# Block two's attention with two heads at a time on the matrix engine, and the overflow path's copies on another queue

## Chip, core and metric

The kernel runs as one program on one core of a Trainium2 chip. The metric is the device time of one execution in microseconds; lower is better. Engines are named as in the profile: PE is TensorE's matmul side and PEld its weight load, DVE is VectorE, ACT is ScalarE, POOL is GpSimd, and SP is SyncE, which here only issues transfers. A "q" behind a name means the engine's sequencer.

## The reference

Two transformer blocks run one behind the other on 256 tokens of width 1024, batch 1, in float32. Block one mixes an mLSTM with a latent attention and adds a mixture of 32 experts. Block two is what the change is about. It projects the normalised tokens once, and from the pieces computes three attentions with heads of 64 columns each:

```
y_a = fox_attention(qa, ka, va, fa)                 # 4 heads, causal, logit plus sum of log f
y_b = dilated_attention(qb, kb, vb, dil_slopes)     # 6 heads in 3 groups (window, stride), joint softmax
y_c = nsa_attention(qc, kc_, vc_, ksl, vsl, kwn, vwn, gc, ...)  # 6 heads, 2 key groups: 3 parts
merged = g[0]*(y_a @ w_pa) + g[1]*(y_b @ w_pb) + g[2]*(y_c @ w_pc)
x = x + merged @ w_o
x = x + conv_ffn(rms_norm_2(x, norm2_g), w_up, conv_w, conv_b, w_down)
```

In the NSA part each head has three products of its own: selected keys, window keys, and 15 compressed keys made from blocks of 32 tokens. Each is weighted by a gate.

## The kernel before

Weights stream from HBM through rings of 1 MB tiles, all on SyncE's queue. Most products are made in three passes on rounded halves of weight and activation (lines 316, 317 and 321, or 338 to 340): ScalarE rounds a weight tile (line 300), VectorE forms the rest (line 301), TensorE multiplies. A planner puts the instructions of each engine in order by its own estimates of their times; a few orders are set by hand.

**Block one's experts** run in 8 groups of 4 (lines 1072 to 1148). Tokens above an expert's 32 places are taken by `overflow`, whose body stands under an If on the largest count (line 1247). In the measured run no expert has that many, and the body is skipped; engines pass the If all the same. Its weights come by copies that SyncE issues (line 1256), into the tiles with the tag "eo", which line 1137 also writes in the ordinary path.

**Block two's `attend`** (from line 1320) has eight PSUM banks: three with the tag "a" for projections, two "s" for scores, two "y" for outputs, one "t" for transposes and sums. `prods` loads one of 21 weight chunks and multiplies it into one "a" bank; `proj` reads the bank into queries, keys, or gates. Queries of two heads share a tile of 128 rows (64 rows each). Keys are stored twice, once for each head, with zeros in the other head's 64 rows (`kz`, `kn`; lines 1365, 1366, 1392 to 1397), so that a product over all 128 rows gives one head's scores. For each head in turn:

1. scores: a product of 128 columns and one of 256 (lines 427 and 429; for NSA's second key set lines 1596 and 1597),
2. bias or slope added by VectorE, then `softmax` (lines 438 to 446) on VectorE and ScalarE,
3. `turn`: three transposes (line 454) into the "t" bank and one copy by ScalarE (line 455),
4. `pv`: the values' products (lines 459 and 460) into 64 of the 128 rows of a "y" bank.

There are 4 such heads for FoX, 6 for dilated (all scores of three groups for one half first, then one softmax over them) and 6 for NSA, which pass steps 1 to 4 for two key sets each: 22 passes of steps 3 and 4. Chunks 11 to 20 of the projection don't depend on the attention and are placed by the planner between its steps; the last two (`LATE`) stand by hand behind the last NSA score product (`tc.issue_after`, line 1643). The merged projections (`wp`) and the output projection (`wo2`) follow, then `ffn`.

Of the kernel before, what the change touches and what calls it, by code (L numbers as in the profile page):

```python
# [222 lines left out]
class Prog:  # L223
# [1016 lines left out]
    def overflow(self, tm, pm, psum, hn, W, pos, thr, most):  # L1240
# [6 lines left out]
        with tc.If(most > CAP, preferred_fallthrough_block=False):  # L1247
# [72 lines left out]
    def attend(self, ei):  # L1320
# [12 lines left out]
        def mps(tag, bufs):  # L1333
            return psum("a", 3)
# [11 lines left out]
        parts = [psum("s", 2) for _ in range(2)]  # L1346
# [4 lines left out]
        pt = psum("t", 1)  # L1351
# [9 lines left out]
        kz = pa.tile([P, 5, 2, T], F32, name="kz")  # L1361
        kn = pa.tile([P, 2, 527], F32, name="kn")
        for p in range(2):
            o = slice(64 * (1 - p), 64 * (1 - p) + 64)
            g.memset(kz[o, :, p], 0.0)
            g.memset(kn[o, p], 0.0)

        def prods(ch, h):
            w = self.load(I["w2a"][ch] if ch < 20 else I["w2a1"][0])
            if ch == CAT:  # L1370
                self.const(self.pc, "tab2", ["pos0", "dil00", "cmp0", "cmp1", "cval0", "hsel", "wfg", "ck2", "cv2"] +
                           [f"dil{i}0" for i in range(3)], nc.sync)
                self.rows(self.pc, "row2", ["bv", "bfg"], nc.sync)
                self.const(self.pc, "tri", ["negu", "cmask"], nc.sync)
            pp = psum("a", 3)
            for j in range(w.shape[-1] // D):
                self.tile_a(w[:, j * 1024:(j + 1) * 1024], h, [(pp[:, j * T:(j + 1) * T], 0, KD)])
            return pp

        def place(n, o):  # L1380
            b = self.co("b2", n, 1)
            lo, up = slice(0, 64), slice(64, 128)
            if n < 2:
                for gi, r in enumerate((lo, up)):
                    a.activation(zt[lo, 2 * n + gi], o[r], AF.Identity, bias=b[r])
                    a.activation(zt[up, 2 * n + gi, 0:T - 1], o[r, 1:T], AF.Identity, bias=b[r])
            elif n in (2, 3, 6, 7, 8, 12, 13, 14):
                i = {2: 0, 3: 1, 6: 2, 7: 3, 8: 4, 12: 5, 13: 6, 14: 7}[n]
                a.activation(q_[:, i], o, AF.Identity, bias=bs[:, n:n + 1], scale=0.125)
            elif n in (4, 5, 9, 10, 11):  # L1390
                i = {4: 0, 5: 1, 9: 2, 10: 3, 11: 4}[n]
                v.tensor_scalar(out=kz[lo, i, 0], in0=o[lo], scalar1=b[lo], scalar2=None, op0=OP.add)
                v.tensor_scalar(out=kz[up, i, 1], in0=o[up], scalar1=b[up], scalar2=None, op0=OP.add)
            elif n in (15, 16):
                s = slice(0, 256) if n == 15 else slice(271, 527)
                v.tensor_scalar(out=kn[lo, 0, s], in0=o[lo], scalar1=b[lo], scalar2=None, op0=OP.add)
                v.tensor_scalar(out=kn[up, 1, s], in0=o[up], scalar1=b[up], scalar2=None, op0=OP.add)
            else:
                a.activation(gates[:, n - 17], o, AF.Tanh, bias=bh[:, n - 17:n - 16], scale=0.5)
# [76 lines left out]
        for kv in range(2):  # L1476
# [7 lines left out]
            part = psum("a", 3)  # L1484
# [9 lines left out]
            hp = psum("a", 3)  # L1494
# [10 lines left out]
            if kv == 0:  # L1505
                v.scalar_tensor_tensor(out=hu, in0=hu, scalar=1.0, in1=hx, op0=OP.add, op1=OP.mult)
                kp = psum("a", 3)
# [3 lines left out]
                for gi in range(2):  # L1511
                    r = slice(64 * gi, 64 * gi + 64)
                    v.tensor_scalar(out=kn[r, gi, 256:271], in0=kp[r, 0:NCMP], scalar1=0.5, scalar2=None, op0=OP.mult)
            else:
# [4 lines left out]
                vp = psum("a", 3)  # L1519
# [7 lines left out]
        gb = [psum("s", 2) for _ in range(2)]  # L1527
# [13 lines left out]
        def finish(Pn, yo, vs):  # L1541
            PT = tm.tile([P, 384], F32, name="PT", tag="PT")
            self.turn(Pn, psum("t", 1), PT)
            self.pv(yo, V[:, 0, vs], V[:, 1, vs], PT)

        for i in range(2):
            yp = psum("y", 2)
            for p in range(2):
                hd = 2 * i + p
                S = psum("s", 2)  # L1550
                self.scores(S, [(q_[:, i], kz[:, i, p])])
                Pn = tm.tile([P, 384], F32, name="Pn", tag="Pn")
                v.tensor_tensor(out=Pn, in0=S[:, 0:384], in1=mc[:, hd], op=OP.add)
                self.softmax(Pn, Pn, sm)
                finish(Pn, yp[64 * p:64 * p + 64], slice(hd * 64, hd * 64 + 64))
            self.hilo(yp[:, :T], y[0][:, i], y[1][:, i])
# [3 lines left out]
        halves = (slice(0, 128), slice(128, 384))  # L1560
        for p in range(2):
            Pd = tm.tile([P, 3, 384], F32, name="Pd", tag="big6", bufs=1)
            for gi in range(3):
                S = psum("s", 2)
                self.scores(S, [(q_[:, 2 + gi], kz[:, 2 + gi, p])])
                at = COLS[f"dil{gi}0"][0]
                v.scalar_tensor_tensor(out=Pd[:, gi], in0=self.where["dil00"][:, at:at + 384], scalar=DIL_SLOPES[gi * 2 + p],
                                       in1=S[:, 0:384], op0=OP.mult, op1=OP.add)
            cc = sm.tile([P, 6], F32, name="smc", tag="smc")
            for q, s in enumerate(halves):  # L1570
                v.tensor_reduce(out=cc[:, q:q + 1], in_=Pd[:, :, s], axis=AX.XY, op=OP.max, negate=True)
            for q, s in enumerate(halves):
                a.activation(Pd[:, :, s], Pd[:, :, s], AF.Exp, bias=cc[:, q:q + 1], accum_out=cc[:, 2 + q:3 + q])
            v.tensor_scalar(out=cc[:, 2:4], in0=cc[:, 2:4], scalar1=TINY, scalar2=None, op0=OP.max)
            v.reciprocal(out=cc[:, 4:6], in_=cc[:, 2:4])
            for q, s in enumerate(halves):
                v.tensor_scalar(out=Pd[:, :, s], in0=Pd[:, :, s], scalar1=cc[:, 4 + q:5 + q], scalar2=None, op0=OP.mult)
            for gi in range(3):
                hd = 2 * gi + p
                finish(Pd[:, gi], yp[gi // 2][64 * p:64 * p + 64, (gi % 2) * T:(gi % 2 + 1) * T], slice(512 + hd * 64, 576 + hd * 64))  # L1580
# [8 lines left out]
        for i in range(3):  # L1589
            yp = psum("y", 2)  # L1590
            for gi in range(2):
                hd = i + 3 * gi
                q = q_[:, 5 + i]
                S1, S2 = psum("s", 2), psum("s", 2)
                self.scores(S1, [(q, kn[:, gi, 0:256])])
                mm(S2[:, 0:143], q[:, 0:128], kn[:, gi, 256:399], start=True, stop=True)
                late = mm(S2[:, 143:414], q[:, 128:256], kn[:, gi, 256:527], start=True, stop=True)
                sl = NSA_SLOPES[hd]
                Pn = [tm.tile([P, 384], F32, name="Pn", tag="Pn") for _ in range(2)]
                v.scalar_tensor_tensor(out=Pn[0], in0=pos, scalar=sl, in1=S1[:, 0:384], op0=OP.mult, op1=OP.add)  # L1600
                v.scalar_tensor_tensor(out=Pn[1][:, 0:128], in0=pos[:, 0:128], scalar=sl, in1=S2[:, 15:143], op0=OP.mult, op1=OP.add)
                v.scalar_tensor_tensor(out=Pn[1][:, 128:384], in0=pos[:, 128:384], scalar=sl, in1=S2[:, 158:414], op0=OP.mult, op1=OP.add)
                for qq in range(2):
                    v.scalar_tensor_tensor(out=Pc[:, qq, hd * 15:hd * 15 + 15], in0=self.co(f"cmp{qq}"), scalar=sl,
                                           in1=S2[:, 143 * qq:143 * qq + 15], op0=OP.mult, op1=OP.add)
                yo = yp[64 * gi:64 * gi + 64, :T]
                for b in range(2):
                    self.softmax(Pn[b], Pn[b], sm, gc[:, :, hd * 3 + 1 + b])
                    PT = tm.tile([P, 384], F32, name="PT", tag="PT")
                    self.turn(Pn[b], psum("t", 1), PT)  # L1610
                    vs = 256 + 128 * b + 64 * gi
                    self.pv(yo, V[:, 0, vs:vs + 64], V[:, 1, vs:vs + 64], PT, first=b == 0, last=b == 1)
# [14 lines left out]
        tp = psum("t", 1)  # L1627
# [37 lines left out]
        part = psum("s", 2)  # L1665
        for ch in range(4):
            w = self.load(I["wo2"][ch])
            pp = psum("a", 3)
# [7 lines left out]
        self.sumcol(psum("t", 1), [(part, 4, D)], cols[:, 56:58], tm)  # L1676
# [137 lines left out]
```

## Time and profile before

| | |
|---|---|
| median of 3 runs | 1019.4 us (1016.81 to 1020.24) |
| profiled execution | 1018.99 us |
| its span | 1017.1 us |
| mean granted TensorE clock | 0.970 |
| PE busy | 946.8 us, 93% of the span |
| DVE busy | 611.6 us, 60% |
| ACT busy | 475.4 us, 47% |

The profiled execution is one of its own and not one of the three runs. Busy times of engines overlap, and their shares are means over stages with different limits. In block two the attention lies from about 644 to 760 us of the span, between the first projections (from 556) and the merged ones.

### The profile page before, as it was taken

The page shows a single profiled execution, that of the slowest core. Times are in us where ns is not written, and L with a number is a line of the kernel's source. Part 1 is how long each engine was busy: PE and PEld are TensorE (multiplying, and loading weights), DVE is VectorE, ACT ScalarE, POOL GpSimd, SP SyncE. Part 2 cuts the span into 40 slices and gives each one's busy share as a digit, 9 for nine tenths or more (in the row PEclk, how much of TensorE's full clock was granted, in tenths as well). Part 3 has the DMA queues.
Part 4 walks back from the last instruction along what each step waited for, and adds up shares of the span by engine and source line. Part 5 has one row for each costly group of instructions (what it writes and reads, how often), then busy time and mean ns, then how long its engine had stood idle before and what let it go on. Part 6 is the DMA issues. An engine that isn't in the chain of part 4 may idle for free.

```text
span 1017.1 us, 17796 instructions
## 1 busy us (share of the span) xinstructions
PE 946.8 (93%) x6870; PEld 774.7 (76%) x6870; DVE 611.6 (60%) x1471; ACT 475.4 (47%) x1017; POOL 16.7 (2%) x32
## 2 busy tenths in 40 slices
PE   5899899999999899997598999999999999999995
PEld 2678888999998554443243998789879799999994
DVE  3468699654763423242134884756779688676764
ACT  3446766455542222120114754656654565555553
POOL 0000000000000000000010000000002000000001
PEclk9899899999999799998799999999999999999998
DMA  8967367669568599999899555723324444554501
GB/s 359 399 277 275 119 248 267 231 266 421 183 239 354 201 423 411 419 422 419 351 380 420 224 187 186 271 103 123 127 83 165 148 166 166 172 201 167 200 8 43
DMA packets 37388, 249.77 MB, mean 246 GB/s; under 512 B 4272, under 2 KB 5040, under 8 KB 8368
## 3 DMA queue, kind: packets, MB, share of 16 engines
q1 hardware_dynamic: 37008, 248.01, 63.2%
q8 instruction: 56, 0.92, 0.4%
q10 hardware_dynamic: 288, 0.55, 0.2%
q14 instruction: 36, 0.29, 0.1%
HBM read 247.49 MB, written 1.05 MB: 244 GB/s over the span
## 4 chain that ended last, share of the span: by engine, by line
PE 45%; ACT 2%; DVE 2%; issue 1%; ACTq 0%; DVEq 0%
PE ps_a L316 9%; PE ps_a L317 9%; PE ps_a L321 9%; PE ps_acc L1772 6%; PE ps_gu L1089 1%; PE ps_y L459 1%; PE ps_c L1131 1%; PE ps_dn L1148 1%; PE ps_t L454 1%; PE ps_a L339 1%; PE ps_a L338 1%; PE ps_a L340 1%; PE ps_s L429 1%; PE ps_y L460 0%; PE ps_a L1489 0%
## 5 line engine op out<-in xcount | busy, mean ns | idle before, releaser
L301 DVE TENSOR_TENSOR wlo<-w,whi 128x512 fp32r<-128x512 f32 (+2 forms) x426 | 288.7, 685 | 151.5 <-ACT whi L300 134.9
L300 ACT CAST whi<-w 128x512 fp32r<-128x512 f32 (+2 forms) x426 | 258.1, 611 | 249.8 <-PE ps_a L317 189.4
L316 PE MATMUL ps_a<-hh,whi 128*128 128x256 f32 x304 | 79.9, 294 | 4.9 <-ACT hh L612 3.1
L317 PE MATMUL ps_a<-hl,whi 128*128 128x256 f32 x304 | 79.4, 291 | 0.0
L1132 DVE SCALAR_TENSOR_TENSOR xT<-ps_c,modc,xT 128x256 f32<-128x256 f32 x72 | 33.1, 483 | 72.5 <-PE ps_c L1131 72.3
L316 PE MATMUL ps_a<-h4h,whi 128*128 128x256 f32 x304 | 76.1, 283 | 0.2 <-ACT h4h L343 0.2
L317 PE MATMUL ps_a<-h4l,whi 128*128 128x256 f32 x304 | 76.1, 283 | 0.0
L1089 PE MATMUL ps_gu<-w,xg 128*32 128x512 f32 x512 | 68.8, 618 | 6.5 <-issue 6.5
L316 PEld LDWEIGHTS ps_a<-hh,whi 128*128 128x128 f32 x304 | 60.0, 198 | 9.1 <-ACT hh L612 3.3
L316 PE MATMUL ps_a<-h2h,whi 128*128 128x256 f32 x248 | 63.9, 288 | 0.0
L317 PE MATMUL ps_a<-h2l,whi 128*128 128x256 f32 x248 | 63.6, 287 | 0.0
L317 PEld LDWEIGHTS ps_a<-hl,whi 128*128 128x128 f32 x304 | 60.2, 198 | 2.0 <-issue 1.2
L316 PEld LDWEIGHTS ps_a<-h4h,whi 128*128 128x128 f32 x304 | 58.1, 192 | 1.2 <-ACT h4h L343 0.6
L317 PEld LDWEIGHTS ps_a<-h4l,whi 128*128 128x128 f32 x304 | 58.1, 192 | 0.3
L1131 PE MATMUL ps_c<-PT,eo 128*128 128x256 f32 (+1 forms) x144 | 41.9, 410 | 12.9 <-ACT eo L1137 11.8
L1131 PEld LDWEIGHTS ps_c<-PT,eo 128*128 128x128 f32 (+1 forms) x144 | 24.3, 192 | 37.1 <-ACT eo L1137 16.1
L1072 PEld LDWEIGHTS ps_x<-Ph,hn 128*128 128x128 f32 x256 | 34.1, 199 | 22.4 <-issue 17.6
L321 PE MATMUL ps_a<-hh,wlo 128*128 128x256 f32 x304 | 49.3, 285 | 0.0
L321 PE MATMUL ps_a<-h4h,wlo 128*128 128x256 f32 x304 | 48.7, 283 | 0.0
L316 PEld LDWEIGHTS ps_a<-h2h,whi 128*128 128x128 f32 x248 | 47.4, 191 | 0.7 <-issue 0.4
L1077 ACT ACTIVATE xg<-ps_x,modc,cols 128x128 f32<-128x128 f32 x32 | 14.6, 457 | 70.6 <-PE ps_x L1072 61.1
L317 PEld LDWEIGHTS ps_a<-h2l,whi 128*128 128x128 f32 x248 | 47.4, 191 | 0.2
(521 smaller groups left out, 2049.1 us busy)
## 6 DMA issues: line engine op xcount, KB each, us to landing
w<-in_egu_dram SPq DMA_DIRECT2D x66, 1024.0 KB, 18.4
w<-in_edn_dram SPq DMA_DIRECT2D x33, 1024.0 KB, 19.8
w<-in_up_dram SPq DMA_DIRECT2D x22, 1024.0 KB, 4.7
w<-in_w2a_dram SPq DMA_DIRECT2D x20, 1024.0 KB, 7.0
w<-in_mod_dram SPq DMA_DIRECT2D x19, 1024.0 KB, 7.5
w<-in_win_og_dram SPq DMA_DIRECT2D x12, 1024.0 KB, 6.5
w<-in_dn_dram SPq DMA_DIRECT2D x11, 1024.0 KB, 4.8
w<-in_br_dram SPq DMA_DIRECT2D x8, 1024.0 KB, 12.6
```

The costliest lines, as they stand in the source:

```text
L300: nc.scalar.copy(hi, src)
L301: nc.vector.tensor_tensor(out=lo, in0=src, in1=hi.bitcast(F32), op=OP.subtract)
L316: mm(out, hi[:, s], ah[:, k], start=first, stop=False)
L317: mm(out, hi[:, s], al[:, k], start=False, stop=False)
L321: mm(out, lo[:, s], ah[:, k], start=False, stop=last)
L338: mm(out, ah[:, k, ts], hi[:, s], start=a, stop=False)
L1072: mm(o[:, i * P:(i + 1) * P], hn[:, q, d * P:(d + 1) * P], Phs[b][q], start=q == 0, stop=q == 1)
L1077: a.activation(xgs[0][:, i], o[:, i * P:(i + 1) * P], AF.Identity, scale=ac[:, d:d + 1], bias=modc[:, 24 + d:25 + d])
L1089: mm(gu[32 * j:32 * j + 32], xgs[d // 4][:, d % 4, j * CAP:(j + 1) * CAP], w[:, j * 512:(j + 1) * 512], start=d == 0, stop=d == KD - 1)
L1131: mm(o[:, i * T:(i + 1) * T], eo_[:, (d0 + i) * P:(d0 + i + 1) * P], PT, start=True, stop=True)
L1132: v.scalar_tensor_tensor(out=xT[:, d], in0=o[:, i * T:(i + 1) * T], scalar=g2[:, d:d + 1], in1=xT[:, d], op0=OP.mult, op1=OP.add)
L1772: mm(acc[q][nh], x[:, q * P:(q + 1) * P], y, start=k == 0 and x is ah and y is hi, stop=k == KF - 1 and y is lo)
```

## The change

Heads are handled two at a time. Keys are stored once, without zeros. `scores2` takes two heads' products from the two halves of rows into two banks of one tile. `finish2` transposes both heads into a tile of two banks, copies both with one ScalarE instruction of 768 columns, and issues the values' products of both heads next to each other, each to its half of the output's rows. NSA computes the scores of both heads for the first key set, then of both for the second, then the four softmaxes; `late` is now the last product of the second set. The dilated scores of all groups and both halves go to one tile before the softmaxes.

The tags of banks change: "a" has two banks (each `psum("a", 3)` in `attend` becomes `psum("a", 2)`), "s" and "t" are one tile of two banks each, "y" still has two. Small users move: sums of squares, `gb` and the merged projection's third bank to "s", the last sums to "t" and "y". In `overflow` the weight copies are issued by ScalarE (`a`) instead of SyncE.

```diff
@@ overflow @@
                     def part(name, i):
                         w = tm.tile([P, 512], F32, name="wp", tag="eo")
-                        nc.sync.dma_start(w, self.I[name].rearrange("b i p (j f) -> b j i p f", j=4)[bass.ds(b, 1), j, i]
-                                          .rearrange("o p f -> (o p) f"))
+                        a.dma_start(w, self.I[name].rearrange("b i p (j f) -> b j i p f", j=4)[bass.ds(b, 1), j, i]
+                                    .rearrange("o p f -> (o p) f"))
                         return w
@@ attend @@
+        def psum2(tag):
+            return ps.tile([P, 2, 512], F32, name="ps_" + tag, tag=tag, bufs=1)
...
-        kz = pa.tile([P, 5, 2, T], F32, name="kz")
-        kn = pa.tile([P, 2, 527], F32, name="kn")
-        for p in range(2):
-            o = slice(64 * (1 - p), 64 * (1 - p) + 64)
-            g.memset(kz[o, :, p], 0.0)
-            g.memset(kn[o, p], 0.0)
+        k_ = pa.tile([P, 5, T], F32, name="k_")
+        kn = pa.tile([P, 527], F32, name="kn")
...
-                v.tensor_scalar(out=kz[lo, i, 0], in0=o[lo], scalar1=b[lo], scalar2=None, op0=OP.add)
-                v.tensor_scalar(out=kz[up, i, 1], in0=o[up], scalar1=b[up], scalar2=None, op0=OP.add)
+                v.tensor_scalar(out=k_[:, i], in0=o, scalar1=b, scalar2=None, op0=OP.add)
...
-            outs = [psum("a", 3)[:, :n1 - n0] for _ in range(2)]
+            outs = [psum("a", 2)[:, :n1 - n0] for _ in range(2)]
...
-        def finish(Pn, yo, vs):
-            PT = tm.tile([P, 384], F32, name="PT", tag="PT")
-            self.turn(Pn, psum("t", 1), PT)
-            self.pv(yo, V[:, 0, vs], V[:, 1, vs], PT)
+        rows = (slice(0, 64), slice(64, 128))
+
+        def scores2(q, k, w0=128, w1=256):
+
+            S = psum2("s")
+            for p, r in enumerate(rows):
+                mm(S[:, p, 0:w0], q[r, 0:128], k[r, 0:w0], start=True, stop=True)
+            for p, r in enumerate(rows):
+                x = mm(S[:, p, w0:w0 + w1], q[r, 128:256], k[r, 0:w1], start=True, stop=True)
+            return S, x
+
+        def finish2(Ps, yo, vs, first=True, last=True):
+            tp = psum2("t")
+            for p in range(2):
+                for j in range(3):
+                    te.transpose(tp[:, p, j * P:(j + 1) * P], Ps[p][:, j * P:(j + 1) * P], self.co("ident"))
+            PT = tm.tile([P, 2, 384], F32, name="PT", tag="PT")
+            a.copy(PT, tp[:, :, 0:384])
+            for p, r in enumerate(rows):
+                mm(yo[r, 0:256], V[:, 0, vs + 64 * p:vs + 64 * p + 64], PT[:, p, 0:256], start=first, stop=False)
+            for p, r in enumerate(rows):
+                mm(yo[r, 128:256], V[:, 1, vs + 64 * p:vs + 64 * p + 64], PT[:, p, 256:384], start=False, stop=last)
...
+            q = q_[:, 5 + i]
+            S, _ = scores2(q, kn)
+            Ps = [[tm.tile([P, 384], F32, name="Pn", tag="Pn", bufs=4) for _ in range(2)] for _ in range(2)]
+            for gi in range(2):
+                v.scalar_tensor_tensor(out=Ps[0][gi], in0=pos, scalar=NSA_SLOPES[i + 3 * gi], in1=S[:, gi, 0:384], op0=OP.mult, op1=OP.add)
+            S, late = scores2(q, kn[:, 256:527], 143, 271)
...
+            for b in range(2):
+                for gi in range(2):
+                    hd = i + 3 * gi
+                    self.softmax(Ps[b][gi], Ps[b][gi], sm, gc[:, :, hd * 3 + 1 + b])
+                finish2(Ps[b], yp, 256 + 128 * b, first=b == 0, last=b == 1)
...
-            pp = [psum("a", 3) for _ in range(3)]
+            pp = [psum("a", 2) for _ in range(2)] + [psum2("s")[:, 0]]
```

## Rows read from the trace of the kernel before

**Rows 1.** The page: busy time of each engine, and the chain by engine
```profile
PE 946.8 (93%) x6870; PEld 774.7 (76%) x6870; DVE 611.6 (60%) x1471; ACT 475.4 (47%) x1017; POOL 16.7 (2%) x32
...
PE 45%; ACT 2%; DVE 2%; issue 1%; ACTq 0%; DVEq 0%
```

**Rows 2.** Table by stage: length, busy us of PE, PEld, DVE, ACT, POOL, clock, DMA share
```profile
572.00:600.00 28.00, 28.00 (x236) 28.00 (x236) 27.70 (x71) 19.95 (x42) 0.00 (x0) 1.00 0.40 140
...
664.00:690.00 26.00, 26.00 (x195) 23.57 (x194) 14.99 (x32) 13.84 (x28) 0.00 (x0) 1.00 0.29 101
...
712.00:760.00 48.00, 46.56 (x328) 38.97 (x328) 34.94 (x122) 29.16 (x83) 0.00 (x0) 1.00 0.32 112
```

**Rows 3.** TensorE's instructions by line, 644 to 760 us: count, busy us, mean ns
```profile
L459 PE MATMUL ps_y<-PT,V 128*64 128x256 f32 x44 | 14.2, 405 | 1.0 <-ACT PT L455 0.9
...
L429 PE MATMUL ps_s<-kz,q__5882 128*128 128x256 f32 x20 | 6.0, 380 | 0.0
```

**Rows 4.** TensorE's timeline at one head of NSA: start, duration, line, count
```profile
717.85 0.28 PE L316 MATMUL ps_a<-h2h,whi 128*128 128x256 f32 x1
717.97 0.28 PE L317 MATMUL ps_a<-h2l,whi 128*128 128x256 f32 x1
718.18 0.65 PE L459 MATMUL ps_y<-PT,V 128*64 128x256 f32 x2
...
718.98 0.51 PE L1596 MATMUL ps_s<-kn,q__5882 128*128 128x143 f32 x2
```

**Rows 5.** Chain of work from 757 to 761 us: start, duration, line, count
```profile
758.60 0.68 PE ps_y L1635 x4
```

**Rows 6.** TensorE's timeline at two score products, 662 and 728 us
```profile
662.57 0.39 PE L427 MATMUL ps_s<-kz,q__5882 128*128 128x128 f32 x2
...
663.22 0.33 PE L1521 MATMUL ps_a<-tab,hv 128*128 128x64 f32 x2
...
728.55 0.40 PE L1596 MATMUL ps_s<-kn,q__5882 128*128 128x143 f32 x2
...
729.37 0.27 PE L317 MATMUL ps_a<-h2l,whi 128*128 128x256 f32 x1
```

**Rows 7.** Timeline at 570 us; TensorE at 624 us; line 1467 (ns min/median/max, starts)
```profile
569.95 0.28 PE L316 MATMUL ps_a<-h0h,whi 128*128 128x256 f32 x1
...
570.90 0.60 PE L407 MATMUL ps_t<-tab,nc 128*128 128x128 f32 x4
...
572.84 1.41 DVE L1431 TENSOR_TENSOR os<-ps_a,rr 128x256 f32<-128x256 f32 x4
...
624.25 0.33 PE L338 MATMUL ps_a<-whi,h2h 128*128 128x384 f32 x1
...
L1467 DVE TENSOR_TENSOR V<-ps_a,row x4: 548/620/692, 624.2 to 635.5; 128x512 f32<-128x512 f32 x2, 128x384 f32<-128x384 f32 x2
```

**Rows 8.** VectorE's and ScalarE's instructions by line, 644 to 760 us
```profile
L438 DVE TENSOR_REDUCE smc<-Pn 128x1 f32<-128x128 f32 (+1 forms) x32 | 9.9, 344 | 0.1
L446 DVE TENSOR_SCALAR Pn<-Pn,smc 128x128 f32<-128x128 f32 (+1 forms) x32 | 8.7, 315 | 0.2
...
L455 ACT COPY PT<-ps_t 128x384 f32<-128x384 f32 x22 | 10.5, 478 | 17.1 <-PE ps_t L454 17.1
```

**Rows 9.** VectorE's instructions by line, 556 to 640 us
```profile
L1393 DVE TENSOR_SCALAR kz<-os,small 64x256 f32<-64x256 f32 x3 | 1.1, 354 | 0.0
```

**Rows 10.** What the If's line 1247 issues: ns min/median/max, first to last start
```profile
L1247 SPq EVENT_SEMAPHORE  x8: 17/17/17, 488.4 to 507.0; - x8
...
L1247 ACTq EVENT_SEMAPHORE  x1: 17/17/17, 463.9 to 463.9; - x1
```

**Rows 11.** ScalarE's timeline behind the If; in brackets the idle time before
```profile
480.82 0.46 ACT L1077 ACTIVATE xg<-ps_x,modc,cols 128x128 f32<-128x128 f32 x1 [17.02 <-PE ps_x L1072]
...
504.66 0.58 ACT L1137 COPY eo<-ps_dn 128x512 f32<-128x512 f32 x1 [13.04 <-SPq L1247]
```

**Rows 12.** Engines and DMA from 504 to 512 us
```profile
504.00:512.00 8.00, 6.71 (x29) 3.19 (x30) 2.22 (x5) 1.63 (x3) 0.00 (x0) 0.72 0.25 70
```

More of the change, by code (lines that the diff above doesn't have):

```diff
@@ L1345, in attend @@
         h0 = act("h0")
-        parts = [psum("s", 2) for _ in range(2)]
+        parts = psum2("s")
+        parts = [parts[:, i] for i in range(2)]
         sq8 = pa.tile([P, 24, T], F32, name="sq8", tag="gt")
@@ L1391, in place @@
                 i = {4: 0, 5: 1, 9: 2, 10: 3, 11: 4}[n]
-                v.tensor_scalar(out=kz[lo, i, 0], in0=o[lo], scalar1=b[lo], scalar2=None, op0=OP.add)
-                v.tensor_scalar(out=kz[up, i, 1], in0=o[up], scalar1=b[up], scalar2=None, op0=OP.add)
+                v.tensor_scalar(out=k_[:, i], in0=o, scalar1=b, scalar2=None, op0=OP.add)
             elif n in (15, 16):
                 s = slice(0, 256) if n == 15 else slice(271, 527)
-                v.tensor_scalar(out=kn[lo, 0, s], in0=o[lo], scalar1=b[lo], scalar2=None, op0=OP.add)
-                v.tensor_scalar(out=kn[up, 1, s], in0=o[up], scalar1=b[up], scalar2=None, op0=OP.add)
+                v.tensor_scalar(out=kn[:, s], in0=o, scalar1=b, scalar2=None, op0=OP.add)
             else:
@@ L1483, in attend @@
                         in1=self.co("pe", 8 * hf2, 8).unsqueeze(2).to_broadcast([P, 8, NCMP]), op=OP.add)
-            part = psum("a", 3)
+            part = psum("a", 2)
             for hf2 in range(2):
@@ L1493, in attend @@
             proj(9 + kv, h)
-            hp = psum("a", 3)
+            hp = psum("a", 2)
             for hh in range(2):
@@ L1510, in attend @@
                         mm(kp[64 * gi:64 * gi + 64, 0:NCMP], self.co("ck2", hh * 64, 64), hu[:, hh, gi], start=hh == 0, stop=hh == 1)
-                for gi in range(2):
-                    r = slice(64 * gi, 64 * gi + 64)
-                    v.tensor_scalar(out=kn[r, gi, 256:271], in0=kp[r, 0:NCMP], scalar1=0.5, scalar2=None, op0=OP.mult)
+                v.tensor_scalar(out=kn[:, 256:271], in0=kp[:, 0:NCMP], scalar1=0.5, scalar2=None, op0=OP.mult)
             else:
@@ L1525, in attend @@
         y = act("y2")
-        gb = [psum("s", 2) for _ in range(2)]
+        gb = psum2("s")
+        gb = [gb[:, i] for i in range(2)]
         mc = pa.tile([P, 4, 384], F32, name="mc", tag="zm")
@@ L1539, in attend @@
             a.copy(es2[:, :, 128:256], gs[:, :, 0:128])
-        def finish(Pn, yo, vs):
-            PT = tm.tile([P, 384], F32, name="PT", tag="PT")
-            self.turn(Pn, psum("t", 1), PT)
-            self.pv(yo, V[:, 0, vs], V[:, 1, vs], PT)
+        rows = (slice(0, 64), slice(64, 128))
[17 more added lines that the diff above has]
+                mm(yo[r, 128:256], V[:, 1, vs + 64 * p:vs + 64 * p + 64], PT[:, p, 256:384], start=False, stop=last)
         for i in range(2):
             yp = psum("y", 2)
+            S, _ = scores2(q_[:, i], k_[:, i])
+            Ps = [tm.tile([P, 384], F32, name="Pn", tag="Pn", bufs=4) for _ in range(2)]
             for p in range(2):
[L1549 to L1555, printed above, removed]
+                v.tensor_tensor(out=Ps[p], in0=S[:, p, 0:384], in1=mc[:, 2 * i + p], op=OP.add)
+                self.softmax(Ps[p], Ps[p], sm)
+            finish2(Ps, yp, 128 * i)
             self.hilo(yp[:, :T], y[0][:, i], y[1][:, i])
@@ L1560, in attend @@
         halves = (slice(0, 128), slice(128, 384))
-        for p in range(2):
[L1562 to L1568, printed above, removed]
+        Pd = tm.tile([P, 2, 3, 384], F32, name="Pd", tag="big6", bufs=1)
+        for gi in range(3):
+            S, _ = scores2(q_[:, 2 + gi], k_[:, 2 + gi])
+            at = COLS[f"dil{gi}0"][0]
+            for p in range(2):
+                v.scalar_tensor_tensor(out=Pd[:, p, gi], in0=self.where["dil00"][:, at:at + 384], scalar=DIL_SLOPES[gi * 2 + p],
+                                       in1=S[:, p, 0:384], op0=OP.mult, op1=OP.add)
+        for p in range(2):
             cc = sm.tile([P, 6], F32, name="smc", tag="smc")
             for q, s in enumerate(halves):
-                v.tensor_reduce(out=cc[:, q:q + 1], in_=Pd[:, :, s], axis=AX.XY, op=OP.max, negate=True)
+                v.tensor_reduce(out=cc[:, q:q + 1], in_=Pd[:, p, :, s], axis=AX.XY, op=OP.max, negate=True)
             for q, s in enumerate(halves):
-                a.activation(Pd[:, :, s], Pd[:, :, s], AF.Exp, bias=cc[:, q:q + 1], accum_out=cc[:, 2 + q:3 + q])
+                a.activation(Pd[:, p, :, s], Pd[:, p, :, s], AF.Exp, bias=cc[:, q:q + 1], accum_out=cc[:, 2 + q:3 + q])
             v.tensor_scalar(out=cc[:, 2:4], in0=cc[:, 2:4], scalar1=TINY, scalar2=None, op0=OP.max)
@@ L1576, in attend @@
             for q, s in enumerate(halves):
[L1577 to L1580, printed above, removed]
+                v.tensor_scalar(out=Pd[:, p, :, s], in0=Pd[:, p, :, s], scalar1=cc[:, 4 + q:5 + q], scalar2=None, op0=OP.mult)
+        for gi in range(3):
+            finish2([Pd[:, p, gi] for p in range(2)], yp[gi // 2][:, (gi % 2) * T:(gi % 2 + 1) * T], 512 + 128 * gi)
         self.hilo(yp[0].rearrange("p (j t) -> p j t", j=2), y[0][:, 2:4], y[1][:, 2:4])
@@ L1594, in attend @@
[L1594 to L1597, printed above, removed]
                 sl = NSA_SLOPES[hd]
-                Pn = [tm.tile([P, 384], F32, name="Pn", tag="Pn") for _ in range(2)]
-                v.scalar_tensor_tensor(out=Pn[0], in0=pos, scalar=sl, in1=S1[:, 0:384], op0=OP.mult, op1=OP.add)
@@ L1601, in attend @@
-                v.scalar_tensor_tensor(out=Pn[1][:, 0:128], in0=pos[:, 0:128], scalar=sl, in1=S2[:, 15:143], op0=OP.mult, op1=OP.add)
-                v.scalar_tensor_tensor(out=Pn[1][:, 128:384], in0=pos[:, 128:384], scalar=sl, in1=S2[:, 158:414], op0=OP.mult, op1=OP.add)
+                Pw, Sw = Ps[1][gi], S[:, gi]
+                v.scalar_tensor_tensor(out=Pw[:, 0:128], in0=pos[:, 0:128], scalar=sl, in1=Sw[:, 15:143], op0=OP.mult, op1=OP.add)
+                v.scalar_tensor_tensor(out=Pw[:, 128:384], in0=pos[:, 128:384], scalar=sl, in1=Sw[:, 158:414], op0=OP.mult, op1=OP.add)
@@ L1603, in attend @@
                 for qq in range(2):
                     v.scalar_tensor_tensor(out=Pc[:, qq, hd * 15:hd * 15 + 15], in0=self.co(f"cmp{qq}"), scalar=sl,
[L1605 to L1612, printed above, removed]
+                                           in1=Sw[:, 143 * qq:143 * qq + 15], op0=OP.mult, op1=OP.add)
@@ L1664, in attend @@
         self.h0 = act("h3")
-        part = psum("s", 2)
+        part = psum2("t")[:, 0]
         for ch in range(4):
             w = self.load(I["wo2"][ch])
-            pp = psum("a", 3)
+            pp = psum("a", 2)
             for j in range(2):
@@ L1675, in attend @@
                 self.scaled(self.h0, xT, n, hc)
-        self.sumcol(psum("t", 1), [(part, 4, D)], cols[:, 56:58], tm)
+        self.sumcol(psum("y", 2), [(part, 4, D)], cols[:, 56:58], tm)
     def ffn(self, eo):
```

13 lines of the change are left out of this document (6 added, 7 removed).

## The prediction

> **What bounds the kernel now.** I began with the page's busy times and chain: TensorE is busy 946.8 of 1017.1 us, and the chain that ended last is nearly all TensorE [rows 1]. So an edit pays if it takes time off TensorE where TensorE sets the pace, and costs if it makes TensorE wait. The table by stage then says where that is. In block two's attention (644 to 760 us) TensorE is at 26.00 of 26 us and 46.56 of 48, VectorE and ScalarE far below it [rows 2]. In the projections ahead of it (572 to 600) TensorE has 28.00 of 28, with VectorE at 27.70 close behind. Third, TensorE's lines and its own timeline gave counts and prices of the small products [rows 3 to 6]. Last I looked at the two places where the change moves something else: the turn of the projection's banks near 570 us [rows 7], and the If of the overflow path near 490 us [rows 10 to 12]. All prices are from the one profiled execution, 1018.99 us, which is 0.4 us below the median of 1019.4; the sum is taken from the execution and the forecast put on the median.
>
> **Values' products.** Before, each of 22 heads (NSA's six count twice, once for each key set) issues two matmuls of line 459 and two records of line 460 (x44 is 22 times two [rows 3]). In the timeline the last projection matmul starts at 717.97; such matmuls follow one another at 0.12 us, so the next would start at 718.09, but line 459 starts at 718.18, and the next full-width matmul at 718.98 [rows 4]. One head thus takes 0.89 us of TensorE, 0.09 of it on entering the narrow form. The change issues both heads of a pair next to each other, one on each half of the columns. The trace has that form already: line 1635, two heads on two column halves, four records in 0.68 us [rows 5], where two records of one head last 0.65 [rows 4]. So the second head is nearly free. I take 11 pairs at 0.89 in place of 22 heads: 19.6 to 9.8, **-9.8 us**. If the halves ran one after the other the second head would save only its change of form, 11 times 0.09 or -1; line 1635 speaks against that.
>
> The Trainium skill, "TensorEngine Tiling (Array Packing)", section "Key Properties", says that a change of tiling mode drains TensorE. It speaks against many short stretches of narrow matmuls, and the trace agrees: the 0.09 us on the way in [rows 4].
>
> **Scores.** Sixteen heads (4 FoX, 6 dilated, 6 NSA) take 662.57 to 663.22, 0.65 us each. The second NSA product starts at 728.55; the second projection matmul behind it starts at 729.37, which without the break would be 0.12 after the first, so the pair of products took 729.25 - 728.55 = 0.70 us [rows 6], six times. Together 14.6 us. Before, half of each contraction was zeros; after, two heads stand on two halves of rows, into two banks. No row of this trace has two row halves side by side. Two bounds: side by side, a pair costs one head plus a change of form in and out, about 0.2 (twice the 0.09 of rows 4): 8 x 0.85 + 3 x 0.90 = 9.5, **-5.1 us**; one after the other, 14.6 + 11 x 0.2 = 16.8, +2.2 us. The nearest row is line 1635, the same array cut the other way, which does overlap; I take -5.1.
>
> The Trainium skill, "TensorE: Matmul & The Clock Gate", section "Part 3: Packing small matmuls", says that matmuls on different row groups run concurrently, 3.07 times as fast for four of them. No run here shows it yet; by it the scores would save the -5.1, without it they lose the 2.2.
>
> **One copy for two heads.** The transposes stay (66 of them). ScalarE's 22 copies of line 455, 478 ns each, become 11 of twice the width [rows 8]. ScalarE has 29.16 of 48 us there [rows 2], so this lies beside TensorE: 0.
>
> **What the pair gives back.** Both heads' softmaxes must now be done before a pair's transposes, the scores have one pair of banks instead of two single ones, and the last two projection chunks, held behind the last NSA score, must cover four softmaxes where they covered two. A softmax costs VectorE two reductions of 344 ns and two scalings of 315, 1.3 us [rows 8]. Two more behind the last score are 2.6 us; the wider copy adds up to 0.5 and the second head's reads of the scores about 0.4 by the nearest of these rows. The cover is two chunks; in the stage before, TensorE idles only 1.4 us of 48. I take **+3.5**. Nothing if the chunks still cover it all; at most 9, if all three NSA pairs pay about 3.
>
> **Banks: three to two.** The projections now turn over two banks. At the start, the third chunk's first matmul runs at 569.95, into the third bank; chunk zero's bank is read by line 1431 only from 572.84, two of its four instructions of 0.35 us, so it is free at 573.5 [rows 7]. With two banks TensorE would stand 3.6 us; line 407 and its row of sums can move up into the gap, since TensorE's queue would no longer hold matmuls ahead of it (at most some 1.3 us). I take +2.6. In V, the second pair of groups starts at 624.25, while line 1467 only begins to read the first pair at 624.2, 620 ns each [rows 7]: +0.8 for what it would wait. Elsewhere (compression, merged projections) one short read each: +0.6. Together **+4.0**, bounds 2 to 7.
>
> **Keys without padding.** Each key tile loses one of two writes of 64 partitions (354 ns [rows 9]) and GpSimd its memsets. TensorE is full in that stretch, so 0; at best 1 us, as VectorE is at 27.70 of 28 [rows 2].
>
> **The overflow path's queue.** The body isn't run, but its If is passed. At its line SyncE's queue carries eight semaphore events from 488.4 to 507.0, every other engine that works in the body one, at once [rows 10]. ScalarE's copy of line 1137 waits 13.04 us for them, to 504.66 [rows 11], and TensorE behind it. From 504 to 512 DMA is busy for a quarter of the time, so some 6 us of its 8 are lost [rows 12]. In my forecast the eight stay where they are, or wait just as long elsewhere with nobody behind them that is later than today: 0.
>
> **Sum.** -9.8 - 5.1 + 3.5 + 4.0 = -7.4 us: 1018.99 to 1011.6, on the median **1012.0 us**. With the bounds of the give-backs this case has its own range, 1007 to 1017.
>
> **Rivals.**
> *ScalarE waits at the If (slower).* The eight events stood on the queue that issues the body's copies; that queue is now ScalarE's. ScalarE reached the If near 463.9 [rows 10] and would stand there to 507.0. Its work that began at 480.82 then begins 26 us later; the copy at 504.66 came 23.8 us behind that work's start, 13.04 of it waiting, so it would come at 507.0 + 10.8 + up to 1.5 = 519.3, some 14.6 late. Less up to 3 where TensorE waits anyhow behind it, about +12 (between +5, if weights that land meanwhile let TensorE catch up, and +15). With -7.4: 1024 us. For it: the events sit on the issuing queue today. Against: they may be placed by something else than the queue. It decides the sign from 7.4 us of lateness on.
> *SyncE is freed and nobody waits.* The weights keep flowing across the If, and the lost 6 us [rows 12] come off the block: 1006. Against it: TensorE, not DMA, may set the pace behind the If.
> *Row halves run one after the other.* Scores +2.2 instead of -5.1: 1019, no change.
> *The attention's chain takes it back.* VectorE's part of both heads and the single pair of banks cost the upper 9, banks 5: 1019 - 14.9 + 14 = about 1018.
>
> **Chances.** Forecast 0.40; ScalarE waits 0.30; SyncE freed 0.10; row halves 0.09; chain 0.11. Below 0.3%, 3 us, a measurement of this kernel can't tell a change from none. Faster: 0.37 of the forecast, all 0.10 of SyncE freed, 0.05 of the last two: 0.52. Same: 0.03, 0.04 of the slower rival's low end, 0.11 of the last two: 0.18. Slower: 0.26 and 0.04: 0.30. The range runs from 1006 (SyncE freed) to 1026 (the upper part of the slower rival).
>
> **What would show it.** In the new trace, TensorE's two heads of line 459's successor should span about what one spanned, 0.89 us a pair; the score pair about 0.85; a TensorE wait of 2 to 3 us near 570; a few us of wait at the end of attention; and at the If either eight events on SyncE as today, or on ScalarE with a wait to 507. Score pairs of 1.5 us, or ScalarE idle from 464 to 507, would make the prediction wrong.

## The result and the profile after

The changed kernel takes 1007.0 us (median of 4 runs, 1003.45 to 1009.55) against 1018.11 before on the same chip: ratio 0.9889, 95% interval 0.9871 to 0.9907. Run again later beside the experiments it gave 1008.54 us and 0.9907 (0.9890 to 0.9923). I take the mean of the two ratios, 0.9898, as the measure for the experiments: 10.4 us of 1018. Its profiled execution took 1006.2 us with a span of 1004.4, where that of the kernel before had 1017.1.

The page's busy times, which answer to [rows 1]:

```profile
PE 928.5 (92%) x6870; PEld 761.9 (76%) x6870; DVE 604.9 (60%) x1463; ACT 473.3 (47%) x1006; POOL 13.0 (1%) x28
```

TensorE has as many instructions as before and is busy 18.3 us less. Where, by line, in the attention (count, busy us, mean ns; [rows 3] before):

```profile
L1559 PE MATMUL ps_y<-PT,V 128*64 128x256 f32 x44 | 7.2, 405 | 0.3 <-ACT PT L1557 0.3
L1548 PE MATMUL ps_s<-kn,q__5881 64*128 64x256 f32 (+1 forms) x24 | 4.4, 387 | 0.0
...
L1548 PE MATMUL ps_s<-k__5882,q__5881 64*128 64x256 f32 x20 | 3.0, 377 | 0.0
```

The mean of one of the 44 products of line 1559 is the same 405 ns as before, but together they fill 7.2 us where they filled 14.2: they run side by side. The same holds for the row halves of the scores, which the trace of before couldn't show (20 records of 377 ns in 3.0 us, where [rows 3] has 20 of 380 in 6.0). TensorE's timeline gives the price of a pair:

```profile
659.82 0.65 PE L1559 MATMUL ps_y<-PT,V 128*64 128x256 f32 x4 [0.26 <-ACT PT L1557]
660.31 0.39 PE L1561 MATMUL ps_y<-PT,V 128*64 128x128 f32 x4
660.63 0.87 PE L1555 MATMUL ps_t<-tab,Pn 128*128 128x128 f32 x6
661.43 0.49 PE L1546 MATMUL ps_s<-k__5882,q__5881 64*128 64x128 f32 x4
661.75 0.60 PE L1548 MATMUL ps_s<-k__5882,q__5881 64*128 64x256 f32 x4
662.29 0.43 PE L1517 MATMUL ps_a<-tab,hv 128*128 128x64 f32 x2
```

Two heads' values take 659.82 to 660.63, 0.81 us, and one head took 718.18 to 718.98, 0.80 [rows 4]. Two heads' scores take 661.43 to 662.29, 0.86 us, and one took 0.65 [rows 6], so two took 1.30.

The attention also ends earlier within its stage. Before, the last addition of NSA's parts (line 1636) stood behind the last projection, and the last score product (line 1597) 11 us ahead of that projection's end:

```profile
739.98 0.62 PE L1597 MATMUL ps_s<-kn,q__5882 128*128 128x271 f32 x2
...
751.43 0.64 PE L321 MATMUL ps_a<-h2h,wlo 128*128 128x256 f32 x4
```
```profile
L1636 DVE TENSOR_TENSOR yc<-yc,ps_y x3: 415/420/421, 759.3 to 760.5; 128x256 f32<-128x256 f32 x3
```

Now the last addition (line 1648, 737.4) stands ahead of the last projection (742.73), and the last score product 30 us ahead of it:

```profile
712.54 0.72 PE L1548 MATMUL ps_s<-kn,q__5881 64*128 64x271 f32 x2
```
```profile
L1648 DVE TENSOR_TENSOR yc<-yc,ps_y x3: 420/420/422, 733.6 to 737.4; 128x256 f32<-128x256 f32 x3
```
```profile
742.73 0.64 PE L321 MATMUL ps_a<-h2h,wlo 128*128 128x256 f32 x4
743.21 0.28 PE L316 MATMUL ps_s<-y2h,whi 128*128 128x256 f32 x1
```

The wait that two banks cost at the first turn (the third chunk's first matmul, [rows 7]) with the read that it waits for, and the If ([rows 10]):

```profile
571.52 0.36 PE L316 MATMUL ps_a<-h0h,whi 128*128 128x256 f32 x1 [1.34 <-DVE os L1429]
```
```profile
570.63 1.41 DVE L1429 TENSOR_TENSOR os<-ps_a,rr 128x256 f32<-128x256 f32 x4
```
```profile
L1247 SPq EVENT_SEMAPHORE  x8: 17/17/17, 487.8 to 506.0; - x8
...
L1247 ACTq EVENT_SEMAPHORE  x1: 17/17/17, 463.0 to 463.0; - x1
```

The eight events are on SyncE still, though the body's copies are now issued by ScalarE, which passes the If at 463.0 (463.9 before).

How much TensorE works and how much it waits, in three stretches of both kernels: from 556 us to the first score product of the attention, on to the end of the attention (behind its last addition before, behind the last projection now), and on to the sums of the norm ahead of `ffn`. First before, then now (columns as in [rows 2]):

```profile
556.00:645.00 89.00, 88.51 (x679) 82.11 (x677) 66.80 (x158) 53.13 (x107) 0.00 (x0) 1.00 0.60 221
645.00:762.00 117.00, 114.42 (x846) 98.25 (x844) 79.57 (x246) 68.81 (x179) 0.00 (x0) 1.00 0.35 127
762.00:812.60 50.60, 48.35 (x365) 43.42 (x365) 41.37 (x67) 27.15 (x51) 6.06 (x7) 1.00 0.45 157
```
```profile
556.00:645.10 89.10, 86.97 (x676) 81.85 (x676) 62.65 (x150) 52.27 (x106) 0.00 (x0) 1.00 0.54 202
645.10:743.20 98.10, 95.53 (x809) 82.77 (x809) 74.79 (x239) 64.87 (x166) 0.00 (x0) 1.00 0.40 142
743.20:799.90 56.70, 52.08 (x402) 47.50 (x400) 43.35 (x70) 28.97 (x55) 5.60 (x7) 1.00 0.48 165
```

The whole way is 256.6 us before and 243.9 now: all of the 12.7 us between the two executions lie here. TensorE's busy time fell by 16.7 us (251.3 to 234.6). Its waits, the rest of each stretch, grew by 4.0: from 0.5 to 2.1 in the projections, from 2.2 to 4.6 behind the attention, and not at all in the attention (2.6 in both).

### The profile page after: what moved, and what is told of

Read it like the earlier page. It is cut to its first block, busy times and chain, and to the rows that moved or that the text cites. A ratio compares the mean times of both kernels' runs of the same rounds, so it can differ in the third digit from the quotient of the medians.

```text
span 1004.4 us, 17784 instructions
## 1 busy us (share of the span) xinstructions
PE 928.5 (92%) x6870; PEld 761.9 (76%) x6870; DVE 604.9 (60%) x1463; ACT 473.3 (47%) x1006; POOL 13.0 (1%) x28
```

## The experiments

Ratios are to the kernel before, with 95% intervals; the changed kernel's is 0.9898.

**Scores of both heads on one row half.**

```diff
-                mm(S[:, p, 0:w0], q[r, 0:128], k[r, 0:w0], start=True, stop=True)
+                mm(S[:, p, 0:w0], q[rows[0], 0:128], k[rows[0], 0:w0], start=True, stop=True)
...
-                x = mm(S[:, p, w0:w0 + w1], q[r, 128:256], k[r, 0:w1], start=True, stop=True)
+                x = mm(S[:, p, w0:w0 + w1], q[rows[0], 128:256], k[rows[0], 0:w1], start=True, stop=True)
```

> The changed kernel, but both heads of a score pair read the same half of rows (0 to 64) of queries and keys, so head 1 gets head 0's scores: as many matmuls of the same shapes, only not on two halves. If the gain is TensorE's own time, the pairs no longer run side by side and the scores cost what the other bound of the prediction said, 16.8 us in place of 9.5: 7 us slower than the changed kernel, about 4 below the kernel before. If the gain came from the chain of softmaxes and copies, TensorE's extra time hides and it stays 11 below.

Ratio 0.9946 (0.9931 to 0.9961), 4.9 us slower than the changed kernel. TensorE's timeline in this run:

```profile
662.31 0.71 PE L1546 MATMUL ps_s<-k__5882,q__5881 64*128 64x128 f32 x4
662.86 1.03 PE L1548 MATMUL ps_s<-k__5882,q__5881 64*128 64x256 f32 x4
663.82 0.43 PE L1517 MATMUL ps_a<-tab,hv 128*128 128x64 f32 x2
```

A pair now takes 1.51 us instead of 0.86. Eleven pairs are 7.2 us of TensorE's time, most of which is in the end time. The array's time decides, not the chain. This run is not the kernel before at that place: two heads took 1.30 us there, not 1.51, so its 4.9 us can't be read as the pairing's gain.

**Values' products head by head.**

```diff
-            for p in range(2):
+            PT = tm.tile([P, 2, 384], F32, name="PT", tag="PT")
+            for p, r in enumerate(rows):
                 for j in range(3):
                     te.transpose(tp[:, p, j * P:(j + 1) * P], Ps[p][:, j * P:(j + 1) * P], self.co("ident"))
-            PT = tm.tile([P, 2, 384], F32, name="PT", tag="PT")
-            a.copy(PT, tp[:, :, 0:384])
-            for p, r in enumerate(rows):
+                a.copy(PT[:, p], tp[:, p, 0:384])
                 mm(yo[r, 0:256], V[:, 0, vs + 64 * p:vs + 64 * p + 64], PT[:, p, 0:256], start=first, stop=False)
-            for p, r in enumerate(rows):
                 mm(yo[r, 128:256], V[:, 1, vs + 64 * p:vs + 64 * p + 64], PT[:, p, 256:384], start=False, stop=last)
```

> The changed kernel with the values' products head by head: transposes, a copy of 384 columns and both products of head 0, then the same for head 1; score pairs and banks as changed. If the gain is TensorE's time, 22 times 0.89 us return in place of 11: 9.8 us slower than the changed kernel, about 1 below the kernel before. If what counts is that both heads' softmaxes and copies overlap, which stays, it is within 3 us of the changed kernel.

Ratio 0.9988 (0.9975 to 1.0000), 9.2 us slower than the changed kernel. The products fill 14.2 us again:

```profile
L1558 PE MATMUL ps_y<-PT,V 128*64 128x256 f32 x44 | 14.2, 405 | 1.0 <-ACT PT L1557 1.0
```

**One copy per head, and two copies cut by columns.** The run above also splits ScalarE's copy, so two controls split it alone.

```diff
-            a.copy(PT, tp[:, :, 0:384])
+            for p in range(2):
+                a.copy(PT[:, p], tp[:, p, 0:384])
```

> The changed kernel with two ScalarE copies of 384 columns per pair in place of one of 768; products still paired. The control for the run with the products head by head: if that run lost TensorE's time, this one stays within 2 us of the changed kernel. If it lost by the chain through ScalarE's copies, this one loses several us too.

Ratio 0.9962 (0.9947 to 0.9976): 6.5 us slower. By its time alone that is the second case, the chain through ScalarE. But the trace shows that most of the products weren't paired any more; in seven of the eleven pairs a projection matmul stands between the two heads, as here:

```profile
L1560 PE MATMUL ps_y<-PT,V 128*64 128x256 f32 x44 | 12.0, 405 | 0.0
```
```profile
696.84 0.65 PE L1560 MATMUL ps_y<-PT,V 128*64 128x256 f32 x2
697.41 0.38 PE L317 MATMUL ps_a<-h2l,whi 128*128 128x256 f32 x1
697.73 0.43 PE L1560 MATMUL ps_y<-PT,V 128*64 128x256 f32 x1
```

The likely reason is that with a copy per head the first head is ready first by the planner's times, so that the planner fills the time between. So a second control:

```diff
-            a.copy(PT, tp[:, :, 0:384])
+            a.copy(PT[:, :, 0:256], tp[:, :, 0:256])
+            a.copy(PT[:, :, 256:384], tp[:, :, 256:384])
```

> The changed kernel with two copies per pair again, but cut by columns: the first brings 256 columns of both heads, the second 128, so both heads' products become ready together and stand next to each other on TensorE in the planned order. If the run with one copy per head lost 6 us because the planner set the products of a pair apart, this one stays within 2 us of the changed kernel. If a second copy's time on ScalarE costs it, this one is some 6 us slower too.

Ratio 0.9891 (0.9876 to 0.9906), that of the changed kernel, with the products at 7.2 us again. The number of copies costs nothing that can be seen; what cost the 6.5 us is that the two heads no longer stood next to each other on TensorE.

**Two projection banks in the kernel before.**

```diff
-            pp = psum("a", 3)
+            pp = psum("a", 2)
...
-            pp = [psum("a", 3) for _ in range(3)]
+            pp = [psum("a", 2) for _ in range(2)] + [psum("s", 2)]
```

> The kernel before with two projection banks in place of three (the merged projection's third bank from the scores' tag) and nothing else. By the prediction's term 4.0 us slower than before (2.6 at the first turn, 0.8 in V, 0.6 elsewhere). By what the changed kernel's trace shows (a wait of 1.34 us at the first turn, V some 1 us late) about 2. A rival: the planner fills the gap with other work and it costs nothing that can be measured.

Ratio 1.0033 (1.0021 to 1.0045): 3.4 us slower, 2.1 to 4.6 by the interval. The third case is out; 4.0 fits, and 2 isn't far outside. TensorE's waits in this run:

```profile
570.29 0.35 PE L316 MATMUL ps_a<-h0h,whi 128*128 128x256 f32 x1 [1.34 <-DVE os L1431]
...
783.32 0.55 PE L316 MATMUL ps_a<-mg2h,whi 128*128 128x256 f32 x1 [3.37 <-DVE mm L1657]
```

1.34 us at the first turn, and 3.37 behind the merged projection, a place to which the prediction had given a part of 0.6. The kernel before waited 0.69 us in that stage:

```profile
775.91 0.36 PE L316 MATMUL ps_a<-y2h,whi 128*128 128x256 f32 x1 [0.69 <-DVE mm L1657]
```

**The queue back on SyncE.**

```diff
-                        a.dma_start(w, self.I[name].rearrange("b i p (j f) -> b j i p f", j=4)[bass.ds(b, 1), j, i]
+                        nc.sync.dma_start(w, self.I[name].rearrange("b i p (j f) -> b j i p f", j=4)[bass.ds(b, 1), j, i]
```

> The changed kernel with the overflow path's copies back on SyncE's queue. The eight events of the If stood on SyncE in both traces, so by the prediction's term nothing changes: within 1 us of the changed kernel, 11 below before. If the queue matters somewhere that the If's rows don't show, it moves by 3 us or more.

Ratio 0.9897 (0.9871 to 0.9923): no difference that can be seen.

**Unpadded keys in the kernel before, one head at a time.**

```diff
-                self.scores(S, [(q_[:, i], kz[:, i, p])])
+                self.scores(S, [(q_[rows[p], i], k_[rows[p], i])])
...
-                v.tensor_scalar(out=kz[lo, i, 0], in0=o[lo], scalar1=b[lo], scalar2=None, op0=OP.add)
-                v.tensor_scalar(out=kz[up, i, 1], in0=o[up], scalar1=b[up], scalar2=None, op0=OP.add)
+                v.tensor_scalar(out=k_[:, i], in0=o, scalar1=b, scalar2=None, op0=OP.add)
```

> The kernel before with unpadded keys only: each head's scores from its own 64 rows, still one head at a time, three projection banks, products as before. If the scores' gain needs two heads side by side, nothing is gained here: from 0 to +4 us against before (22 score pairs that change the form, at 0.2 us). If the shorter contraction, the lost writes or the lost memsets were what gained, it is 3 to 6 us below before.

Ratio 1.0027 (1.0013 to 1.0041): 2.7 us slower. The halved contraction by itself costs; of the two forms tried here, only two at once gain. The lost writes and memsets gain nothing that can be seen.

**No chunk held behind the last scores** (`LATE = 2` becomes `LATE = 0`).

> The changed kernel with no projection chunk held behind the last score product (2 before). The prediction's give-back of 3.5 us supposed that these two chunks must cover the pairs' last softmaxes: then, without them, TensorE waits there and this is at least 3 us slower than the changed kernel. If the attention now ends well ahead of the last projection by the planner's own order, as the trace shows (last product of the compressed part near 736, last projection at 743), nothing changes.

Ratio 0.9907 (0.9875 to 0.9939): no difference that can be seen. In the trace TensorE has the same order as in the changed kernel, at times 0.2 us apart (last addition at 737.2 and 737.4): the planner sets these chunks behind the last score product by itself. So this run shows that the hold no longer does anything. It does not show what would happen without chunks behind the last scores.

**The merged projection in two sets of banks.**

```diff
+            if ch % 2:
+                pp = [psum("y", 2) for _ in range(2)] + [psum2("t")[:, 0]]
+            else:
+                pp = [psum("a", 2) for _ in range(2)] + [psum2("s")[:, 0]]
```

> The changed kernel, with the merged projection's odd chunks in the two output banks and the transposes' tile, its even ones where they are: a chunk no longer waits until the chunk before it is read. The trace of the changed kernel shows TensorE waiting 1.6 us for that read; if these waits are what the banks still cost there, this is 1 to 2 us faster than the changed kernel; if the end of that stage is set by the additions behind it, no change.

Ratio 0.9900 (0.9884 to 0.9917): no gain. TensorE finishes the merged products earlier and then waits in one piece:

```profile
774.53 0.80 PE L316 MATMUL ps_a<-mg2h,whi 128*128 128x256 f32 x2 [3.30 <-ACT mg2h L343]
```

**More banks for the early chunks and V.**

```diff
-            pp = psum("a", 2)
+            pp = psum("y" if ch == 2 else "a", 2)
...
-            outs = [psum("a", 2)[:, :n1 - n0] for _ in range(2)]
+            outs = [psum("y" if n0 else "a", 2)[:, :n1 - n0] for _ in range(2)]
```

> The changed kernel once more, as the measure for the two runs beside it on the same chip: 11 us below before.

> The changed kernel, with the third early projection chunk and V's second pair of groups in the output banks (tag y), which are free there: three, then four banks in turn. If the 1.3 us wait near 570 us and V's delay of about 1 us are what two banks cost at these places, this is 1.5 to 2.5 us faster than the changed kernel. If other work sets the pace of these stages (VectorE is full from 572 to 600 us), it is within 1 us.

The changed kernel beside it gave 0.9907, as told above; this one 0.9910 (0.9896 to 0.9924). The wait near 570 us is gone from the trace and the end is where it was. The 1.3 us came back later as other waits (2.2 and 1.7 us around the compression, where the changed kernel waits 1.8 and 0.5).

**One VectorE instruction moved.** The end of the merged stage in the changed kernel, on VectorE and TensorE:

```profile
773.71 0.69 DVE L1763 TENSOR_SCALAR row<-row 128x1024 f32<-128x1024 f32 x1 [0.95 <-DMA row<-in_row_dram]
774.32 0.68 DVE L344 TENSOR_TENSOR mg2l<-mm,mg2h 128x512 fp32r<-128x512 f32 x1
```
```profile
775.05 0.39 PE L317 MATMUL ps_a<-mg2l,whi 128*128 128x256 f32 x1 [1.92 <-DVE mg2l L344]
```

The last norm's gains are scaled by line 1763, which waits 0.95 us for its own transfer and then runs 0.69, ahead of `mg2l`, for which TensorE stands 1.92 us. In the kernel before the same scaling (line 1751) stood behind `mg2l`, and TensorE had no such wait:

```profile
786.94 0.69 DVE L344 TENSOR_TENSOR mg2l<-mm,mg2h 128x512 fp32r<-128x512 f32 x1
787.55 0.69 DVE L1751 TENSOR_SCALAR row<-row 128x1024 f32<-128x1024 f32 x1
```

The run holds it behind the output projection's last addition:

```diff
-                v.scalar_tensor_tensor(out=xT[:, n], in0=o, scalar=0.5, in1=xT[:, n], op0=OP.mult, op1=OP.add)
+                self.done = v.scalar_tensor_tensor(out=xT[:, n], in0=o, scalar=0.5, in1=xT[:, n], op0=OP.mult, op1=OP.add)
...
-        v.tensor_scalar(out=gf, in0=gf, scalar1=float(D ** 0.5), scalar2=None, op0=OP.mult)
+        with tc.issue_after(self.done.ins):
+            v.tensor_scalar(out=gf, in0=gf, scalar1=float(D ** 0.5), scalar2=None, op0=OP.mult)
```

> The changed kernel with one VectorE instruction moved: the scaling of the last norm's gains (line 1763), which waits for its own transfer, is held behind the output projection's last addition. In both profiles of the changed kernel it stands ahead of the last part of the merged activation (line 344), and TensorE waits 1.9 and 2.2 us for that. If this is the remaining give-back of the faster attention, the wait shrinks to under 1 us, the granted clock no longer falls behind it, and the kernel is 1.5 to 4 us faster than the changed one (about 13 below before). If VectorE's other work there (it is full from 764 to 772 us) sets the end anyway, no change.

Ratio 0.9879 (0.9861 to 0.9896), median 1004.8 us, the lowest of all kernels here. Its TensorE at the same place:

```profile
773.36 0.39 PE L317 MATMUL ps_a<-mg2l,whi 128*128 128x256 f32 x1 [0.26 <-DVE mg2l L344]
```

The wait fell from 1.92 to 0.26 us. The interval overlaps that of the changed kernel, so the 2 us between them are shown in the trace and not beyond doubt in the time.

## Why the prediction was right, and where its sizes were off

**Values' products.** Forecast -9.8. A pair takes 0.81 us where a head took 0.80, and undoing it cost 9.2. Right. The Trainium skill, "TensorEngine Tiling (Array Packing)", section "Key Properties", says that a change of tiling mode drains TensorE. That did no harm that the time shows: the products now stand in 11 narrow stretches in place of 22. What the prediction didn't see is the condition: the planner must leave the two heads adjacent. It does so where the copies make both heads ready at once (one of 768 columns, or two cut by columns), and mostly not with a copy per head. The copy was costed at nothing.

**Scores.** Forecast -5.1, with 0.85 us a pair; measured 0.86 a pair where two heads took 1.30. Eleven times the difference of 0.44 is 4.8 us of TensorE's time. The end times agree, if nothing else differs: the run with the values head by head has the score pairs and two banks and is 1.2 us below the kernel before, where two banks alone are 3.4 above, which leaves 4.6 to the scores. The choice between the two bounds, by the column halves of [rows 5], held. The run with one row half shows the other bound (1.51 us a pair; the prediction named 1.5), and the run with unpadded single heads shows that half a contraction alone is a loss of 2.7 us, inside the 0 to 4 that its expectation allowed for changes of form.

**TensorE's time as a whole.** The two gains are 14.9 us in the forecast; TensorE's busy time fell by 16.7 from 556 us to the norm ahead of `ffn`. Where the other 1.8 us went is open: the transposes of two heads now stand together too, and no run takes that apart.

**Banks.** Forecast +4.0, measured +3.4 by themselves. The size is right and the places are not. At the first turn it is 1.34 us in place of 2.6, because VectorE's order moved too: it reads chunk zero's bank from 570.63, where the prediction had it at 572.84 as before. The larger wait (3.37 us in that run, 0.69 in the kernel before) is behind the merged projection. Lifting the first wait alone gained nothing. So the sum over single places, each as if nothing else could wait instead, came out by luck in part.

**What the pair gives back.** This is the term that was mis-sized: forecast +3.5, and TensorE's waits in the attention are 2.6 us before and now, so nothing of it was measured there. The step that failed is that two chunks must cover four softmaxes at the end of the attention. I had kept the place of the last score product as before, 11 us ahead of the last projection. The planner now sets it at 712.54, 30 us ahead, so the last addition comes at 737.4 with projections still to run, and holding two chunks back no longer does anything. Which part of the change brings the scores forward isn't shown.

Two smaller waits stand in its place. One is that of the single pair of score banks, which the prediction named: the second FoX pair waits until VectorE, which first does the compression's work, has read the first.

```profile
646.54 0.22 DVE L1501 TENSOR_TENSOR hu<-hu,hx 128x60 f32<-128x60 f32 x1
646.68 1.01 DVE L1568 TENSOR_TENSOR Pn<-ps_s,mc 128x384 f32<-128x384 f32 x2
```
```profile
647.84 0.49 PE L1546 MATMUL ps_s<-k__5882,q__5881 64*128 64x128 f32 x4 [1.80 <-DVE hu L1504]
```

Line 1568 reads the first pair from 646.68 to 647.69, and the second pair's scores start at 647.84, after 1.80 us. The bracket names `hu` because that instruction ended last by the profile; the score product doesn't use `hu`, so I put the wait down to the read. That is an argument from the kernel: the two end 0.13 us apart, and no run separates them. The other wait is that for `mg2l` above, 1.92 us: in the planner's new order the scaling stands ahead of it.

**The If.** Forecast 0, measured 0; the rival that put ScalarE behind the eight events, at 0.30 the strongest, is out: they don't follow the queue that issues the copies. What decides their place isn't shown. The other rivals fell too: the row halves run side by side, SyncE wasn't freed, and the chain took nothing back.

**The number.** 1012.0 was forecast and 1007.0 came: inside the range, at the lower end of what the forecast allowed for its own case (1007), and as a number nearer to the rival with SyncE freed (1006). Only the traces and the run with the queue back tell the two apart. In the two profiled executions the gains were 1.8 us larger than forecast (16.7 against 14.9) and the waits 3.5 smaller (4.0 against 7.5). The executions are 12.7 us apart and the medians 11.1, or 10.4 by the mean of both ratios, where 7.4 were forecast; the kernel before also came 1.3 us lower than in the forecast (1018.11 against 1019.4). The ratios of the experiments can't simply be added to split this, since undoing one part does not give back the kernel before at that place, as with the one row half.

## What to carry to other kernels

Two matmuls that each fill half of the array's rows or columns can cost little more than one: here 0.81 us against 0.80 for column halves, and 0.86 against 0.65 for row halves. For the column halves the runs show the condition: they must be neighbours on TensorE. Price such pairs from a trace's own pair if there is one, and make both ready at once, or a planner may part them. A half contraction alone gained nothing here. Do not take the planner's order as fixed when you sum waits place by place: the first turn, the end of the attention and the wait for `mg2l` were missed by that. When a change lets a planner reorder, look next at the order on the engines that feed TensorE: an instruction that waits for its own transfer can stand ahead of the one that TensorE needs.

## What the hardware showed that was not expected

The same changed kernel, in two profiled executions, had nearly the same wait before 648 us (1.80 and 1.94 us; TensorE busy 2.20 and 2.06 us of 4) and two different clocks behind it. Stretches of the first execution, then of the second (columns as in [rows 2]):

```profile
644.00:648.00 4.00, 2.20 (x21) 1.79 (x22) 3.54 (x12) 1.88 (x5) 0.00 (x0) 1.00 0.89 336
648.00:652.00 4.00, 3.49 (x52) 1.95 (x51) 3.66 (x16) 1.86 (x8) 0.00 (x0) 1.00 0.31 92
```
```profile
644.00:648.00 4.00, 2.06 (x20) 1.65 (x20) 3.54 (x12) 1.89 (x6) 0.00 (x0) 0.93 0.86 342
648.00:652.00 4.00, 4.00 (x36) 2.20 (x40) 3.65 (x16) 1.86 (x8) 0.00 (x0) 0.50 0.02 10
652.00:656.00 4.00, 4.00 (x34) 2.91 (x27) 2.58 (x12) 3.82 (x13) 0.00 (x0) 0.72 0.74 266
...
776.00:780.00 4.00, 2.49 (x11) 2.49 (x12) 1.89 (x4) 0.62 (x1) 0.00 (x0) 0.64 0.45 182
```

In the second, TensorE fell to the lower level (0.50, 1.2 GHz) after that wait and again after the wait near 775 us; its span was 1008.2 us against 1004.4. The first waits ended at 647.84 and 647.79 us, and the values' products that the first execution starts at 659.82 start 2.16 us later in the second:

```profile
661.98 0.65 PE L1559 MATMUL ps_y<-PT,V 128*64 128x256 f32 x4 [0.26 <-ACT PT L1557]
```

A wait of 2 us can thus cost more than its length, and not in each execution: the run without chunks held back, which has the same order, waited 1.85 and 2.00 us at the two places and kept 1.00 behind both. In the run with the instruction moved the wait near 773 us is 0.26 us and the clock stayed at 1.00 there; one profile of it doesn't settle how often that holds.
